# Placing small products behind dense ones, an earlier rotary table, and stores on another queue, in a one-layer hybrid attention and RWKV-7 block

## The chip, the cores and the metric

The kernel runs on one core of a Trainium2 chip. The metric is the device time of one execution in microseconds (us), lower is better. In the text and the rows PE is TensorE, the matrix engine; DVE is VectorE, ACT is ScalarE, POOL is GpSimd and SP is SyncE, which in this kernel only issues transfers. SPq and POOLq are the queues of transfers that SP and POOL issue.

## The reference, cut to what matters

One decoder layer over 1024 tokens of width 1024, in float32. One wide projection of the normed input feeds two token mixers that stand side by side: multi-head latent attention (8 heads, with low-rank queries and keys and a rotary part) and an RWKV-7 recurrence (8 heads of 64). Sixteen blocks of gate columns of the same projection merge them.

```
z = rmsnorm(x, g_mix) @ w_in              # MLA columns | r k v, low-rank w a g | gates
c_q, c_kv, k_pe = split(z_mla)            # 384 | 256 | 32 columns
q  = rmsnorm(c_q) @ w_uq;  kv = rmsnorm(c_kv) @ w_ukv
cos, sin = rope_tables(positions)         # rotary tables, applied to 32 columns of q and k
o_mla = causal_attention(q, k, v) @ w_o_mla

w = decay(w0 + tanh(w_lo) @ w2);  a = sigmoid(a0 + a_lo @ a2);  g = sigmoid(g_lo) @ g2
kk = k * k_k / norm(k * k_k)              # per head
S_t = S_{t-1} diag(decay_t) + (S_{t-1} a_t) b_t^T + v_t k_t^T ;  y_t = S_t r_t
o_rwkv = (groupnorm(y) + bonus) * g @ w_o_rwkv

x = x + sigmoid(gate_1) * o_mla + sigmoid(gate_2) * o_rwkv
x = x + relu(rmsnorm(x) @ w_up)**2 @ w_down
x = x + sigmoid(rmsnorm(x) @ w_gate) * (p @ w_proj);  out = rmsnorm(x) * g_final
```

## The kernel before, in words

Float32 matrices are split into a rounded high part and a low remainder, and each product is taken as three: high by high, low by high, high by low. One block of 128 columns of the wide projection is then 48 products of 128x512, three for each of 8 slices of the inner dimension and two halves of the tokens. These are the **dense** products (tiles `psd`, and `pg` for gate blocks of the recurrence). Around each block the raw weights arrive (`wr`), ACT rounds them (`wh`, line 215), DVE takes the remainder (`wl`, line 216), and at its end ACT and DVE read the block out of the accumulator.

The stages follow one another on PE:

- **First stage** (0 to 143 us of the profiled execution): the norm and transposes of x, the key columns, the low-rank columns, then the low-rank products (`lora`, line 466: 12 results, each read out by ACT into a tile `sa` and stored), then the norm of the keys: `n2`, its square root `sn`, DVE's reciprocal `rn` and a Newton step (lines 477 to 488), rounded by ACT into `rns`. Four small products `nb` (line 502) spread it over the keys, `kz`, which are stored in `kh_d`. Tiles `kz`, `n2`, `sn`, `rn`, `sa`, `zs` share 13 buffers, tag `ta`.
- **Early stage** (143 to 368 us). The generator `early(g)`, for each of 8 groups of 128 tokens, loads what the first stage stored and makes the small products `L` (line 670). `inverse(b)`, for each half of the sequence, loads them as `U` and inverts 32x32 triangles by forward substitution on DVE, a chain of 62 instructions (`prd`, `X`, lines 689 and 690) in which each waits for the one before it. It stores the result, loads it transposed (`mt`), and DVE transposes it once more (`x`, line 707). Then PE runs 128 small products `y` (lines 714 and 722) in 16 groups of 8, ACT copying between the groups. `norm_latent` needs a small product `st`, some DVE arithmetic, and a transpose `rT` (line 293).
- **Recurrence stage** (368 to 590 us): for each of 16 chunks products `pc` in three steps, each followed by a copy or a sum on DVE and ACT that the next step waits for.
- **Attention stage** (590 to 836 us): `latents` loads five stored tiles (`latf`, 512 KB each) and splits them into `chi` and `clo`; `rope_tables` computes the rotary table in 13 DVE instructions and a sine on ACT; then values (`v`), queries (`qp`) and keys (`kn`), and the heads.
- Then the merge (to 1033 us), the channel mixer (to 1660 us), and the gated embedding with the final norm (`gated`, line 1679).

Chunks of work are Python generators that yield an estimate of their cost. `weave` draws from several in turn so that their costs grow in given proportions, and this sets the order of the instructions on every engine. The dense blocks are the filler: `main` (all columns that are still to be made) is woven with the small work at weights `T_EARLY` 203, `T_LATE` 600, `T_MAIN` 306 and `T_REST` 40. A larger number yielded by a small chunk lets more dense products follow it. Each engine works through its own instructions in order. `together` keeps a few small products next to one another. All stores go through SP's queue, which also carries nearly all loads.

```
first = chainit(*(early(g) for g in range(4)))
second = chainit(weave([(inverse(0), 40), (chainit(*(early(g) for g in range(4, 8))), 22)]), inverse(1))
run(weave([(chainit(first, second), T_EARLY), (main, T_MAIN)], lead=True))
```

## Time and profile before

| | |
|---|---|
| median of 3 runs | 1764.86 us (1764.24 to 1766.14) |
| the profiled execution | 1766.65 us, of which the span 1764.9 us |
| PE busy | 1689.4 us, 96% of the span |
| DVE, ACT, POOL busy | 1190.9, 850.9 and 263.6 us |
| mean granted TensorE clock | 0.987 |

PE is the bound: what counts is the time in which it is idle, and the time at a clock below 1.00. Other engines matter where PE waits for them. The granted clock is given as a share of 2.4 GHz; 0.50 is 1.2 GHz.

### The profile page before, as it was taken

To read this page: it belongs to the slowest core of one execution; us is meant where nothing else is said; L and a number is where in the kernel's file an instruction comes from. 1 tells how busy PE (TensorE), PEld (TensorE's weight loads), DVE (VectorE), ACT (ScalarE), POOL (GpSimd) and SP (SyncE) were. 2 spreads that over 40 slices of the span, in tenths; PEclk is the share of its full clock that TensorE was granted. 3 is DMA by queue.
4 is the path that set the end of the run, shared out by engine and by line. 5 is a ranking of instruction groups with operands and counts; after the bars stand their busy time and mean duration, and the time that the engine had idled before them with its cause. 6 is when DMAs were issued, how large, how long until landed. Compare 5 with 4: busy or idle time off the path is not lost.

```text
span 1764.9 us, 27006 instructions
## 1 busy us (share of the span) xinstructions
PE 1689.4 (96%) x10492; PEld 1374.2 (78%) x10492; DVE 1190.9 (67%) x1923; ACT 850.9 (48%) x1482; POOL 263.6 (15%) x206
## 2 busy tenths in 40 slices
PE   7999999889999999998999999999999999999997
PEld 6877877667777877777888887888888888888876
DVE  6446695858777578887364378555658787786656
ACT  5553333244444366676244156555556444353365
POOL 2000000000000022222000203333332333332000
PEclk9999999979999999999999999999999999999999
DMA  6257774744553510015353324545558755462213
GB/s 198 72 199 216 199 213 109 194 110 127 162 143 102 178 44 25 25 61 191 107 165 99 111 115 144 167 133 164 165 181 258 234 167 155 152 189 66 72 42 126
DMA packets 241839, 246.12 MB, mean 139 GB/s; under 512 B 48977, under 2 KB 186800, under 8 KB 241712
## 3 DMA queue, kind: packets, MB, share of 16 engines
q1 hardware_dynamic: 239792, 239.39, 44.3%
q0 software_dynamic: 1760, 4.76, 0.8%
q8 instruction: 82, 1.34, 0.3%
q14 instruction: 45, 0.37, 0.1%
q10 hardware_dynamic: 160, 0.27, 0.0%
HBM read 162.31 MB, written 81.53 MB: 138 GB/s over the span
## 4 chain that ended last, share of the span: by engine, by line
PE 69%; DVE 14%; issue 6%; DMA 4%; ACT 4%; POOL 1%; SPq 1%; DVEq 0%; ACTq 0%; POOLq 0%
PE psX L1394 18%; PE psd L225 18%; PE psY L1394 9%; PE pg L1660 5%; PE psZ L1394 5%; PE pg L610 2%; DVE prd L689 1%; DMA r<-rkv_d 1%; PE po L1147 1%; PE k L234 1%; DVE wl L216 1%; DMA a<-sa_d 1%; DVE xb L319 1%; DVE X L690 1%; PE pT L1130 1%
## 5 line engine op out<-in xcount | busy, mean ns | idle before, releaser
L1394 PE MATMUL psX<-xb,sw 128*128 128x512 f32 x768 | 177.5, 389 | 2.2 <-ACT hid L1497 1.1
L1394 PE MATMUL psX<-hb,sw 128*128 128x512 f32 x768 | 176.8, 389 | 0.0
L1394 PEld LDWEIGHTS psX<-xb,sw 128*128 128x128 f32 x768 | 144.0, 188 | 32.9 <-ACT hid L1497 1.6
L1394 PEld LDWEIGHTS psX<-hb,sw 128*128 128x128 f32 x768 | 144.1, 188 | 29.9
L319 DVE TENSOR_TENSOR sw<-sw,sw 128x512 fp32r<-128x512 f32 x128 | 94.3, 741 | 55.3 <-ACT sw L318 55.0
L318 ACT CAST sw<-sw 128x512 fp32r<-128x512 f32 x128 | 79.4, 620 | 103.7 <-PE psX L1394 37.4
L215 ACT CAST wh<-wr 128x1024 fp32r<-128x1024 f32 (+2 forms) x67 | 57.0, 855 | 139.0 <-PE psd L225 120.6
L225 PE MATMUL psd<-xh,wh 128*128 128x512 f32 x384 | 122.8, 399 | 0.5 <-ACT yn L888 0.5
L225 PE MATMUL psd<-xl,wh 128*128 128x512 f32 x384 | 122.2, 397 | 0.0
L216 DVE TENSOR_TENSOR wl<-wr,wh 128x1024 fp32r<-128x1024 f32 (+2 forms) x67 | 68.2, 1020 | 47.8 <-PE psd L225 29.2
L318 ACT CAST sw<-wr 128x512 fp32r<-128x512 f32 x96 | 59.3, 622 | 72.9 <-PE psX L1394 38.7
L225 PE MATMUL psd<-xh,wl 128*128 128x512 f32 x384 | 92.0, 390 | 0.0
L1660 PE MATMUL pg<-wg,g 128*128 128x512 f32 x384 | 91.2, 393 | 0.0
L319 DVE TENSOR_TENSOR sw<-wr,sw 128x512 fp32r<-128x512 f32 x96 | 82.3, 857 | 12.1 <-ACT sw L318 12.0
L1394 PE MATMUL psY<-xb,sw 128*128 128x512 f32 x384 | 89.6, 389 | 0.0
L1394 PE MATMUL psY<-hb,sw 128*128 128x512 f32 x384 | 89.6, 389 | 0.0
L225 PEld LDWEIGHTS psd<-xh,wh 128*128 128x128 f32 x384 | 72.7, 191 | 17.0 <-ACT yn L888 1.0
L225 PEld LDWEIGHTS psd<-xl,wh 128*128 128x128 f32 x384 | 73.1, 191 | 15.8
L225 PEld LDWEIGHTS psd<-xh,wl 128*128 128x128 f32 x384 | 72.0, 188 | 15.4
L1394 PEld LDWEIGHTS psY<-hb,sw 128*128 128x128 f32 x384 | 72.1, 188 | 15.0
L1394 PEld LDWEIGHTS psY<-xb,sw 128*128 128x128 f32 x384 | 72.1, 188 | 15.0
L318 ACT CAST hb<-braw 128x1024 fp32r<-128x1024 f32 x56 | 58.7, 1048 | 51.1 <-DMA braw<-hid_d 19.1
(411 smaller groups left out, 3743.0 us busy)
## 6 DMA issues: line engine op xcount, KB each, us to landing
hid_d<-hid SPq DMA_DIRECT2D x112, 256.0 KB, 4.2
braw<-hid_d SPq DMA_DIRECT2D x56, 512.0 KB, 4.4
wr<-in_w_in_dram SPq DMA_DIRECT2D x35, 512.0 KB, 5.2
wr<-in_w_ffn_up_dram SPq DMA_DIRECT2D x32, 512.0 KB, 5.1
wr<-in_w_ffn_down_dram SPq DMA_DIRECT2D x32, 512.0 KB, 4.0
gate_d<-gt SPq DMA_DIRECT2D x16, 512.0 KB, 3.1
gate<-gate_d SPq DMA_DIRECT2D x16, 512.0 KB, 3.7
xt<-in_x_dram SPq DMA_DIRECT2D x8, 512.0 KB, 8.3
```

The source lines that it names most:

```text
L215: A.copy(dst(wh), src)
L216: V.tensor_tensor(dst(wl), src, dst(wh).bitcast(F32), ALU.subtract)
L225: T.matmul(acc[:, h, :], lhsT=wt[:, k, :], rhs=r[k][:, h * 512:h * 512 + 512], start=wt is wh and k == 0 and ri == 0, stop=wt is wl and k ...
L234: T.matmul(acc, lhsT=wt[:, k, :], rhs=r[k][:, sl], start=wt is wh and k == 0 and ri == 0, stop=wt is wl and k == kb - 1)
L318: A.copy(hi, src)
L319: V.tensor_tensor(lo, src, hi.bitcast(F32), ALU.subtract)
L610: T.matmul(acc, lhsT=wt[:, k, :], rhs=r[k][:, hs], start=wt is wh and k == 0 and ri == 0, stop=wt is wl and k == NB - 1)
L689: V.tensor_tensor(pv, X[:, 0:t, 0:t], U[:, 0:t, t].unsqueeze(1).to_broadcast([P, t, t]), ALU.mult)
L690: V.tensor_reduce(X[:, 0:t, t], pv, AX.X, ALU.add)
L1130: T.transpose(out=tp_[:, b * P:(b + 1) * P], in_=prs[i][:, (4 * g + b) * P:(4 * g + b + 1) * P], identity=ident)
L1394: T.matmul(acc, lhsT=w[:, wl_, j, :], rhs=part(b, xl_, j), start=start and s == 0, stop=key == LAST[bank] and s == len(steps) - 1, skip_gr ...
L1660: T.matmul(acc, lhsT=l[k][:, ts], rhs=r, start=first and i == 0, stop=last and i == 2)
```

## The change

- **Behind dense products.** `behind_dense()` makes the first of a few small products follow the dense step that was last written ahead of it. `together` uses it, and now also holds the products of `early`, of `inverse` (`y`) and `sc` of the recurrence; the transpose in `norm_latent` uses it too.
- **More dense work ahead of the inverse's products.** `inverse` yields 12 in place of 3 before its products, and a step of the recurrence yields 2 at one place in place of two yields of 1.
- **First stage.** The low-rank products become a generator that is woven with the dense block that followed them, and with the rotary table, which moves here from the attention stage. The table is stored (`tab_d`) and loaded again in attention.
- **Latents.** The statistics of `norm_latent` become `latent_rstd`, with dense work between it and the transpose.
- **Attention.** 26 slots are touched first in another order, the five loads `latf` have a slot each (two before), and `rope_keys` stands ahead of `latents`.
- **Stores.** 104 stores move from SP's queue to POOL's.
- **Tail.** `gated` runs a square root of one column on ACT after its second sigmoid, so that the table of functions is loaded there.

```diff
+    def behind_dense():
+        return tc.issue_after(dense_last[0])
...
     def together(*mms):
-            first = mms[0]()
+            with behind_dense():
+                first = mms[0]()
             with tc.issue_after(first.ins):
                 for f in mms[1:]:
-                    last = f()
-            return last
+                    f()
...
+        def low_rank():
+            for which in range(3):
+                for j in range(4):
...
                     t = ta("sa")
                     if which < 2:
                         A.activation(t, flat(acc), AF.Sigmoid, bias=pcol(("w0", "a0")[which], j))
-                        nc.sync.dma_start(sa_d[which, cs, :], t)
+                        nc.gpsimd.dma_start(sa_d[which, cs, :], t)
...
+                    yield 1.7
+        def rope_tables():
+            freq_sb = cp.tile([P, 3], F32, name="freq_sb")
+            nc.sync.dma_start(freq_sb, freq)
+            posi, kf, ang = ta("posi"), ta("kf"), ta("ang")
+            nc.sync.dma_start(posi.bitcast(I32), positions.broadcast_to([P, S]))
+            yield 1
+            V.tensor_copy(ang, posi.bitcast(I32))
+            V.tensor_scalar(ang, ang, freq_sb[:, 0:1], None, ALU.mult)
...
+            for c in (c1, c2, 2 * math.pi - c1 - c2):
+                V.scalar_tensor_tensor(ang, kf, -c, ang, ALU.mult, ALU.add)
+                yield 1
...
+            with tc.issue_after(lora_last[0].ins):
+                A.activation(ang, ang, AF.Sin)
+            V.tensor_scalar(ang, ang, freq_sb[:, 1:2], None, ALU.mult)
+            nc.sync.dma_start(tab_d, ang[64:128])
...
-        run(dense(w_in, 0, NB, MLA_COLS, RV0 * P, xh, xl, evac_rv))
+        tables = rope_tables()
+        run(weave([(dense(w_in, 0, NB, MLA_COLS, RV0 * P, xh, xl, evac_rv), 20.6), (low_rank(), 24), (until(tables, 8), 8)]))
...
+        run(tables)
...
         def latent_cols():
             q = dense(w_in, 0, NB, 0, QR, xh, xl, evac_c)
             yield from dense(w_in, 0, NB, QR, KVR, xh, xl, evac_c, m0=3)
-            yield from until(q, 12)
-            yield from norm_latent((3, 4), KVR, "g_kv", 0)
+            yield from until(q, 8)
+            r = latent_rstd((3, 4), KVR)
+            yield from until(q, 8)
+            yield from norm_latent(r, (3, 4), "g_kv", 0)
...
             def inverse(b):
...
-                yield 3
+                yield 12
                 for c in range(8):
                     y2 = psa((P, 4, CH), s="y2")
-                    for j in range(4):
-                        for h in range(2):
...
+                    together(*[lambda j=j, Rt=Rt, Rb=Rb: T.matmul(y2[Rb, j, 0:32], lhsT=lr[Rt, c * 4 + j, :], rhs=x0[Rt, c * 4 + j, :], start=True, stop=True)
+                               for j in range(4) for Rt, Rb in tops])
...
                 if next_mms:
                     put_values(Wn)
-                yield 1
+                yield 2
...
-                nc.sync.dma_start(fm(yb_d[0], g), hi.bitcast(F32))
+                nc.gpsimd.dma_start(fm(yb_d[0], g), hi.bitcast(F32))
...
+        for i in (14, 15, 6, 7, 2, 3, 4, 5, 21, 10, 11, 0, 1, 8, 12, 16, 9, 13, 17, 18, 19, 20, 22, 23, 24, 25):
+            slot(i)
...
-                    t = slot((12, 13)[n % 2], F32, "latf")
+                    t = slot((12, 13, 19, 20, 24)[n], F32, "latf")
                     nc.sync.dma_start(t, lat_d[m])
...
-            prep = chainit(latents(), lazy(rope_tables), value_weights(), values(0, V0, psa_v), queries(0, psv))
+            prep = chainit(lazy(rope_keys), latents(), value_weights(), values(0, V0, psa_v), queries(0, psv))
...
             A.activation(t, acc, AF.Sigmoid, scale=r1[tb])
+            if n:
+                A.activation(warm, warm, AF.Sqrt)
```

Three places show how instructions move. Lines are those of the kernel in question.

**The key's norm and the low-rank products, ACT and DVE.** On ACT before, the read-outs `sa` of all low-rank products stand ahead of the norm (`n` and its root `sn`), and the rounding `rns` comes two dense read-outs later:

```order
L472 COPY sa_1015<-lora_1008 128x1024
L472 COPY sa_1025<-lora_1018 128x1024
L478 COPY n_134_1028<-kst_618 8x512
L478 COPY n_134_1028<-kst_619 8x512
L480 ACT_TABLE_LOAD
L480 ACTIVATE sn_1029<-n_134_1028 8x1024
L215 CAST wh_1227<-wr_1225 128x1024
L386 ACTIVATE zs_1098<-psd_1049,omu 128x1024
L215 CAST wh_1353<-wr_1351 128x1024
L487 CAST rns<-rn_1030 8x1024
```

On ACT now, the root stands ahead of all twelve read-outs, and `rns` between the fifth and the sixth:

```order
L531 ACTIVATE sn_926<-n_110_925 8x1024
L215 CAST wh_1250<-wr_1248 128x1024
L490 ACT_TABLE_LOAD
L490 ACTIVATE sa_956<-lora_951,pc_rest 128x1024
L490 ACTIVATE sa_974<-lora_969,pc_rest 128x1024
L490 ACTIVATE sa_994<-lora_989,pc_rest 128x1024
L490 ACTIVATE sa_1010<-lora_1005,pc_rest 128x1024
L490 ACTIVATE sa_1023<-lora_1018,pc_rest 128x1024
L538 CAST rns<-rn_927 8x1024
L490 ACTIVATE sa_1037<-lora_1032,pc_rest 128x1024
L490 ACTIVATE sa_1054<-lora_1049,pc_rest 128x1024
```

On DVE now, instructions of the rotary table (`ang`, `kf`) alternate with those that lead from the reciprocal to the finished `rn`, which `rns` reads:

```order
L532 RECIPROCAL rn_927<-sn_926 8x1024
L504 CAST ang_963<-posi_961 128x1024
L533 TENSOR_TENSOR sn_926<-rn_927 8x1024
L505 TENSOR_SCALAR ang_963<-ang_963,freq_sb 128x1024
L534 TENSOR_TENSOR sn_926<-sn_926,n_110_925 8x1024
L506 TENSOR_SCALAR kf_962<-ang_963 128x1024
L535 TENSOR_SCALAR sn_926<-sn_926 8x1024
L507 TENSOR_SCALAR kf_962<-kf_962 128x1024
L536 TENSOR_TENSOR rn_927<-rn_927,sn_926 8x1024
L512 SCALAR_TENSOR_TENSOR ang_963<-kf_962,ang_963 128x1024
L537 TENSOR_SCALAR rn_927<-rn_927 8x1024
```

Five table instructions now stand between the reciprocal and the end of the norm.

**The second inverse's products, PE.** Before, the 128 products `y` follow 212 dense ones and stand with no dense product among them:

```order
L225 MATMUL psd_2924<-xh_171,wl_2921 128x512 x2
L225 MATMUL psd_2924<-xh_172,wl_2921 128x512 x2
L714 MATMUL y_351_2803<-x_348_2774,lr_2775 32x32
L714 MATMUL y_353_2833<-x_348_2774,lr_2775 32x32
L714 MATMUL y_351_2803<-x_348_2774,lr_2775 32x32 x7
L714 MATMUL y_353_2833<-x_348_2774,lr_2775 32x32 x7
L722 MATMUL y_351_2803<-mt_1198,y2s_2812 32x32 x8
L722 MATMUL y_353_2833<-mt_1198,y2s_2842 32x32 x8
L714 MATMUL y_355_2859<-x_348_2774,lr_2775 32x32 x8
```

Now they follow 281 dense products, and each group of 8 is followed by one to six more:

```order
L231 MATMUL psd_2917<-xh_172,wl_2914 128x512 x2
L231 MATMUL psd_2917<-xh_173,wl_2914 128x512 x2
L231 MATMUL psd_2975<-xh_166,wh_2971 128x512 x2
L231 MATMUL psd_2975<-xl_174,wh_2971 128x512 x2
L765 MATMUL y_369_2980<-x_356_2867,lr_2868 32x32 x8
L231 MATMUL psd_2975<-xh_167,wh_2971 128x512 x2
L231 MATMUL psd_2975<-xl_175,wh_2971 128x512
L774 MATMUL y_369_2980<-mt_1221,y2s_2989 32x32 x8
L231 MATMUL psd_2975<-xl_175,wh_2971 128x512
L231 MATMUL psd_2975<-xh_168,wh_2971 128x512 x2
L231 MATMUL psd_2975<-xl_176,wh_2971 128x512 x2
L765 MATMUL y_371_3010<-x_356_2867,lr_2868 32x32 x8
```

**The loads at the start of attention, SP.** Before, the first two `latf` loads come right after the stores `yb_d` of the recurrence's last result, and PE has 140 dense products between the transposes of that result and the first `v`:

```order
L895 DMA yb_d<-yh_5723 128x4x128
L896 DMA yb_d<-yl_5724 128x4x128
L989 DMA latf_5755<-lat_d 128x1024
L989 DMA latf_5787<-lat_d 128x1024
L943 DMA posi_5889<-in_positions_dram 128x1024
L115 DMA wr_6397<-in_w_ukv_dram 128x2x256
L1038 DMA uq_6576<-in_w_uq_dram 128x3x192
L989 DMA latf_5809<-lat_d 128x1024
```

Now the five stand together behind the load `uq_6606`, which waits for DVE's second `wl` of the weights `wr_6090`, and that for the last dense product of the stage. PE has 18 dense products between those transposes and the first `v`:

```order
L940 DMA g_5903<-g_d 128x4x128
L1070 DMA uq_6606<-in_w_uq_dram 128x3x192
L991 DMA tab_5955<-tab_d 64x1024
L993 DMA kpr_5967<-kpr_d 64x1024
L1021 DMA latf_5980<-lat_d 128x1024
L1021 DMA latf_5994<-lat_d 128x1024
L1021 DMA latf_5998<-lat_d 128x1024
L1021 DMA latf_6002<-lat_d 128x1024
L1021 DMA latf_6006<-lat_d 128x1024
```

The dense products that stood there are among those that now stand earlier.

## Rows read from the trace of the kernel before

**Rows 1.** Windows of PE: us, busy (instructions), granted clock, DMA share, GB/s.

```profile
98.00:117.00 19.00, 17.30 (x68) 0.91 0.80 310
...
345.00:374.00 29.00, 16.37 (x287) 0.59 0.73 173
...
400.00:540.00 140.00, 126.96 (x1684) 1.00 0.55 149
...
621.00:640.00 19.00, 16.81 (x68) 0.91 0.29 85
```

**Rows 2.** Timeline of PE: first low-rank product, and the dense one after the last.

```profile
98.71 0.40 PE L466 MATMUL lora<-lora,lw_h 128*128 128x512 f32 x1
...
116.27 0.63 PE L225 MATMUL psd<-xh,wh 128*128 128x512 f32 x2
```

**Rows 3.** Timeline of PE: 75 products of 128x512 in a row.

```profile
1737.67 17.16 PE L1660 MATMUL pg<-wg,g 128*128 128x512 f32 x75
```

**Rows 4.** Timeline of ACT: the key's norm.

```profile
117.42 1.05 ACT L478 COPY n<-kst 8x512 f32<-8x512 f32 x2
118.49 1.28 ACT L480 ACT_TABLE_LOAD   x1
119.78 1.06 ACT L480 ACTIVATE sn<-n 8x1024 f32<-8x1024 f32 x1
```

**Rows 5.** Timeline of DVE: three instructions of the key's norm.

```profile
120.87 6.54 DVE L481 RECIPROCAL rn<-sn 8x1024 f32<-8x1024 f32 x1 [1.69 <-ACT sn L480]
...
128.59 1.21 DVE L482 TENSOR_TENSOR sn<-rn 8x1024 f32<-8x1024 f32 x1
...
132.16 0.68 DVE L484 TENSOR_SCALAR sn<-sn 8x1024 f32<-8x1024 f32 x1
```

**Rows 6.** Timeline of PE: the transpose of the second latent norm.

```profile
236.42 0.27 PE L293 MATMUL rT<-ident,rr 128*8 128x128 f32 x1 [2.47 <-DVE rr L207]
```

**Rows 7.** Timeline of PE: two groups of `y` in the first inverse, one dense product between.

```profile
289.76 0.44 PE L714 MATMUL y<-x,lr 32*32 32x32 f32 x16
...
290.56 0.44 PE L714 MATMUL y<-x,lr 32*32 32x32 f32 x16
```

**Rows 8.** Timeline of PE: the second inverse's first products.

```profile
354.50 0.42 PE L714 MATMUL y<-x,lr 32*32 32x32 f32 x4 [8.64 <-DVE x L707]
```

**Rows 9.** Window of DVE: the second inverse's chain; columns as in the first group.

```profile
287.00:345.00 58.00, 47.08 (x72) 1.00 0.54 149
```

**Rows 10.** Timeline of DVE: a wait inside that chain, its end, the transpose after it.

```profile
302.44 1.23 DVE L216 TENSOR_TENSOR wl<-wr,wh 128x1024 fp32r<-128x1024 f32 x1 [9.07 <-PE psd L225]
...
343.56 1.16 DVE L690 TENSOR_REDUCE X<-prd 128x31 f32<-128x961 f32 x1
...
355.19 1.24 DVE L707 STREAM_TRANSPOSE x<-xc 32x1024 f32<-32x1024 f32 x1 [0.74 <-ACT xc L706]
```

**Rows 11.** Timeline of PE: two waits of the recurrence stage.

```profile
488.19 0.69 PE L852 MATMUL pc<-W,bk 128*64 128x64 f32 x16 [1.34 <-ACT W L848]
...
535.85 0.69 PE L833 MATMUL pc<-W,q 128*64 128x64 f32 x16 [1.34 <-DVE W L859]
```

**Rows 12.** Timeline of PE: the wait at the start of attention.

```profile
632.04 0.47 PE L234 MATMUL kn<-chi,wh 128*128 128x512 f32 x1 [2.19 <-ACT wh L215]
```

**Rows 13.** Timeline of ACT: the rounding of one latent tile.

```profile
599.58 1.05 ACT L318 CAST chi<-latf 128x1024 fp32r<-128x1024 f32 x1 [0.82 <-DMA latf<-lat_d]
```

**Rows 14.** DMA issues: queue, number, KB each, median us to landing.

```profile
sa_d<-sa SPq DMA_DIRECT2D x8, 512.0 KB, 3.0
...
latf<-lat_d SPq DMA_DIRECT2D x5, 512.0 KB, 5.0
...
bh<-yb_d POOLq DMA_DIRECT2D x4, 512.0 KB, 9.1
```

**Rows 15.** Timeline of ACT: the root of the last block's norm.

```profile
1757.84 1.28 ACT L202 ACT_TABLE_LOAD   x1
1759.14 0.20 ACT L202 ACTIVATE rs<-rv 128x1 f32<-128x1 f32 x1
```

155 lines of the change are left out of this document (76 added, 79 removed).

## The prediction, made before the changed kernel was run

> **What bounds the kernel now.** I read the windows of PE first, then PE's timeline for each window in which it is idle or its granted clock is below 1.00, then the queues of the engines that it waits for there. PE is busy for 96% of the span, so the change can only gain where PE stands still or runs at half clock, and each dense product that fills one hole is taken from another place. The number of dense products is the same before and after. One of them advances PE by 0.227 us, (17.16 - 0.16) / 75 [rows 3].
>
> The windows to look at are four [rows 1]: the low-rank products (clock 0.91), the second inverse (16.37 busy of 29.00 us at 0.59), the recurrence stage (126.96 of 140 us) and the start of attention (16.81 of 19 us at 0.91). All times below are on the scale of the profiled execution, 1766.65 us, 1.8 above the median.
>
> **The change part by part** (+ is time saved).
>
> *Second inverse, +19.* The last dense product ends at 345.9; the first `y` starts after a wait of 8.64 us for DVE's transposes [rows 8], and the clock stays at half to about 373.9: 28.0 us. The work done in them, at full clock, is 256 records of `y` at 0.44 / 16 less their start-up, about 5.9 us [rows 7], ten dense products, 2.3, and 0.5 of transposes: 8.7. The loss is 19.3. Why so late? DVE's chain starts at 287.3, stands 9.07 us behind a `wl` that waits for PE, ends at 344.7, and the second transpose ends at 356.4 [rows 10], 11.7 later (a store, a load, copies on ACT). Of DVE's 47.1 busy us there [rows 9] some 43 are the chain, counting off the other work.
>
> In the new order the chain starts when the last dense block of the `r` columns ends, t. It needs 2.5 us of that block's read-out (`wl` and `zs`), 43 of chain, about 7 of other work put among it: `x` is whole at t + 52 + 11.7 = t + 64. PE has 292 dense products and 24 records of the first inverse before the second's first `y`: t + 68. No wait, with 4 us to spare. I take +19; were DVE 9 us slower, the gain would be +14.
>
> *Visits, -3.6.* Between two groups of `y`, 0.80 us apart, stand 0.37 of `y` and one dense product: the mixing costs 0.20 [rows 7]. In the new order there are about 16 such visits more in the second inverse and 7 in the first: -3.6 to -4.6, and -2 if longer stretches between groups cost less.
>
> *First inverse, -3.5.* Its chain now starts after a transpose `rT`, 51 us after the products `nb` end, and its 43 us have some 28 us of other instructions among them, of which, as between 198 and 268 us before, about three quarters count: the end is at 115, plus 2 for waits, and the first transpose of `x` 8.5 later, at 126. PE arrives at about 124 (264 dense, 32 products for the rotary key columns, the small ones). I take 2 us of waiting and 1.5 of half clock; 0 and -8 are the ends.
>
> *The second `rT`, +3.7.* PE waits 2.47 us there for DVE's `rr` [rows 6] and then runs four us at a clock near 0.57, 1.7 more. The statistics now stand 38 dense products and 16 `L` ahead, 9.8 us, as long as DVE's part took (227.0 to 236.4). Ends: 0 and +4.2.
>
> *Low-rank products, -7.6.* Before, 60 products take 17.6 us [rows 2] where 13.6 would do: 4.0 lost. In the new order ACT's rounding `rns` stands ahead of the sixth read-out, and PE has three accumulators. `rns` needs the end of the key's norm. Count from the end of the last `kst`: two copies, a table load and the root, 3.5 us [rows 4], the reciprocal, 6.5, and then not five but ten instructions on DVE, five of them of the table; at 1.21 or 0.68 each they take 8.9 [rows 5]. `rns` is done 20 us after `kst`. PE in that time has 31 dense products (7.0) and five groups of low-rank ones (about 5.5, plus 1.2 for their read-outs of 1.0 each): it stands some 7 us. Then about 2 us are lost at half clock, and 2 before it: 11.6 in all, against 4.0. If the table's instructions cost nothing, the loss would be 6; if stores hold the buffers of `sa`, 16. So -2 to -12.
>
> *Recurrence, +6.* PE is idle for 13.0 of 140 us [rows 1], in waits of one to one and a half us for the copies after each step [rows 11]. The waits for ACT's `W` had two to four dense products ahead of them, and now mostly ten, or six and four with `sc` between: these go, about 5 us and what is like them. One comes: the transposes `yT` now stand ahead of a step and need DVE's `yc`, which has two instructions of 1.2 us ahead of it. Half of the 13; ends 0 and +13.
>
> *Start of attention, -9.7.* Before, PE waits 2.19 us [rows 12] and loses 1.7 to the clock. Now the five `latf` stand on SP behind a load that waits until 0.6 us after the last dense product, t. Four loads are issued by t + 2.3, all eight by t + 4.7. A `latf` takes 5.0 us to land [rows 14], and the eight are 3.4 MB: at 310 GB/s 11 us, at 173 20 us [rows 1]. ACT rounds each in 1.05 [rows 13], DVE takes three instructions for the rotary key first and then 1.2 for each `clo`. So the first `v` starts near t + 8.6, and the last `clo` is there at t + 18. PE has 27 products to do in that time, 6.1 us: idle for 11.9, then 1.7 at half clock as before. 13.6 against 3.9. Ends: -3 (all landed by t + 9) and -18 (last at t + 22).
>
> *Tail, +0.9.* The table load of 1.28 us between the last sum and the root [rows 15] moves ahead of ACT's last square, into 1.49 us in which ACT waits for DVE.
>
> *Stores, 0.* POOL is idle for nearly all of 150 to 625 us, so issuing costs nothing. What a store on its queue takes is not in the trace of before; the nearest rows are 3.0 us on SP's and 9.1 on POOL's for eight loads issued together [rows 14]. I take the lower: most stores come singly. The waits that hang on them (buffers of `sa`, the reload of `kh_d`, `l_d`) then stay as they were.
>
> The Trainium skill speaks here against the change: by "SBUF — State Buffer", section "SBUF: two separate sides", GpSimd writes the descriptors of its transfers itself, and cannot while certain DVE instructions hold the port that the two share, so that such a transfer seems blocked. By it a store issued beside the reciprocal could start as much as 6.5 us later, and the sum would be that of the third rival below. The row of `bh` neither shows nor excludes it.
>
> **Sum:** 19 - 3.6 - 3.5 + 3.7 - 7.6 + 6 - 9.7 + 0.9 = +5.2. 1766.65 - 5.2 = 1761.4, and 1.8 lower on the scale of the median: 1759.6 us.
>
> **The rivals.**
>
> *The holes move and nothing is gained.* The idle time of PE stays what it was, because the filler is the same: the recurrence gives nothing (DVE's own queue holds each step), and the rest of the sum is -0.8: 1765.7 us. For it: the two new holes above are read off the order alone. Against: the hole at 346 us is nearly all loss at half clock, and 4 us of slack speak for it.
>
> *Slower, by the latent loads.* Eight transfers at 173 GB/s, the last `clo` at t + 26: PE idle for 20 us, -18 in place of -9.7: 1768. From -15 on (a last `clo` after t + 23) it decides. For it: the rate at 345 us; against: 310 GB/s at 98 us.
>
> *Slower, by late stores on POOL's queue.* At 9.1 us a store, the third buffer of `sa` comes 1.4 us later, and `kh_d` to `k` to the first `L` 5 us; -8 with the clock: 1768. It decides where stores take over 7 us. For it: the row of `bh`; against: those eight share the bandwidth.
>
> *Much faster.* `rns` doesn't hold the read-outs because DVE gets to the norm sooner, and the latents land by t + 9: +5.6 and +6.7: 1747.
>
> **How the numbers follow.** My forecast 0.40, much faster 0.14, nothing gained 0.22, the two slower ones 0.14 and 0.10. A measurement of this kernel tells about 0.2%, 3.5 us, from no change. The forecast lies 5 us below the median, so a part of its spread lies within 3.5: faster 0.51, same 0.24, slower 0.25. The range, 1746 to 1772, takes in all cases; the likeliest one's own is 1752 to 1766.
>
> **What would show it right or wrong.** Around the second `y` PE should be busy at clock 1.00, with dense products between the groups. In the first stage a wait of about 7 us for ACT's `sa` or `rns` should stand among the low-rank products. At the start of attention several waits for `chi` and `clo`, 10 to 13 us in all, with `latf` issued after the last gate block's `wl`. `rT` should wait less than 1 us. The waits of `pc` for ACT's `W` should be gone, and `yT` should wait for `yc`. The prediction is wrong if the second inverse still waits, if PE passes the low-rank products without a long wait, or if the latents are there when PE wants them.

## The result, and the profile after

The changed kernel takes **1773.82 us** (median of 4 runs, 1772.71 to 1776.1) against 1764.55 us beside it: a ratio of 1.0052 with an interval of 1.0037 to 1.0067, some 9 us slower. Forecast were 1759.6 us, in a range of 1746 to 1772. The execution profiled after has a span of 1772.5 us (before 1764.9).

The windows of PE that answer to [rows 1], and two in which a new hole stands (us, busy, granted clock, DMA share, GB/s):

```profile
98.00:117.00 19.00, 18.25 (x77) 1.00 0.39 138
122.00:132.00 10.00, 6.04 (x14) 0.50 0.47 170
...
345.00:374.00 29.00, 29.00 (x184) 1.00 0.57 155
400.00:540.00 140.00, 137.65 (x1810) 1.00 0.56 156
607.00:627.00 20.00, 7.21 (x17) 0.57 0.85 279
836.00:852.00 16.00, 11.35 (x35) 0.79 0.77 281
```

The second inverse is full at clock 1.00 (16.37 of 29 us at 0.59 before), and the recurrence has lost nearly all its idle time (137.65 of 140 us, before 126.96). The low-rank products, the start of attention and, at 836 us, the merge have holes, in each of them with a part at 0.50, 1.2 GHz. PE's timeline shows what PE waits for there, and at the products `L` and the transpose `rT` of the early stage:

```profile
125.96 0.80 PE L487 MATMUL lora<-lora,lw_h 128*128 128x512 f32 x1 [6.48 <-ACT sa L490]
...
178.80 1.24 PE L722 MATMUL L<-ah,a 64*64 64x64 f32 x32 [3.40 <-DVE a L717]
...
246.28 0.27 PE L310 MATMUL rT<-ident,rr 128*8 128x128 f32 x1 [3.56 <-DVE rr L207]
...
617.49 1.22 PE L1046 MATMUL v<-wvh,chi 128*128 128x512 f32 x2 [10.45 <-ACT chi L335]
621.04 0.80 PE L1046 MATMUL v<-wvh,clo 128*128 128x512 f32 x1 [2.34 <-DVE clo L336]
...
838.09 1.19 PE L231 MATMUL psd<-bh,wh 128*128 128x512 f32 x4 [0.22 <-DMA bh<-yb_d]
840.91 1.20 PE L231 MATMUL psd<-bl,wh 128*128 128x512 f32 x4 [1.63 <-DMA bl<-yb_d]
843.47 1.18 PE L231 MATMUL psd<-bh,wh 128*128 128x512 f32 x4 [1.36 <-DMA bh<-yb_d]
846.09 2.07 PE L231 MATMUL psd<-bl,wh 128*128 128x512 f32 x4 [1.44 <-DMA bl<-yb_d]
```

For the balance I cut both spans at the same products: the last `nb`, the first and the last `y`, the first `v`, the first `s` (the heads' first product), the first product with `bh` and the first with `oh`. The dense products that fill the stretches were moved between them, so what a stretch saved is its length before, less its length after, plus 0.227 us [rows 3] for each dense product that it now holds more, and less for each that it holds fewer.

| stretch | before, us | after, us | dense products | saved, us | forecast |
|---|---|---|---|---|---|
| start to the last `nb` | 142.5 | 150.8 | 288, 288 | -8.3 | -7.6 |
| to the first `y` | 137.1 | 132.8 | 465, 436 | -2.3 | 3.7 - 2 = +1.7 |
| to the last `y` | 87.9 | 107.3 | 255, 391 | +11.5 | 19 - 3.6 - 1.5 = +13.9 |
| to the first `v` | 253.6 | 226.6 | 568, 469 | +4.5 | |
| to the first `s` | 23.9 | 26.7 | 8, 0 | -4.6 | the two: 6 - 9.7 = -3.7 |
| to the first `bh` | 191.6 | 191.6 | none | 0 | 0 |
| to the first `oh` | 43.6 | 52.3 | none | **-8.7** | 0 |
| to the end | 884.7 | 884.4 | none | +0.3 | +0.9 |
| sum | 1764.9 | 1772.5 | 1584, 1584 | -7.6 | +5.2 |

Of the forecast -3.5 for the first inverse, 2 us are a wait that ends with the first `y`, so they stand in the row before. Two rows make up the miss of 12.8 us: the merge, which the prediction did not look at, with 8.7, and the stretch up to the first `y` with 4.0. The misses of the other rows cancel, which is luck.

### The profile page after: what moved, and what is told of

The parts are those of the page before. It is cut to its first block, busy times and chain, and to the rows that moved or that the text cites. A ratio compares the mean times of both kernels' runs of the same rounds, so it can differ in the third digit from the quotient of the medians.

```text
span 1772.5 us, 27095 instructions
## 1 busy us (share of the span) xinstructions
PE 1695.8 (96%) x10492; PEld 1371.0 (77%) x10492; DVE 1189.1 (67%) x1923; ACT 853.5 (48%) x1491; POOL 329.0 (19%) x312
## 4 chain that ended last, share of the span: by engine, by line
PE 65%; issue 18%; DVE 9%; DMA 3%; ACT 2%; POOL 2%; SPq 0%; DVEq 0%; POOLq 0%; ACTq 0%
PE psd L231 19%; PE psX L1426 18%; PE psY L1426 9%; PE pg L1692 5%; PE psZ L1426 5%; PE po L1179 2%; PE pT L1162 1%; PE k L241 1%; DVE nmx L1138 1%; DVE xb L336 1%; PE qp L241 1%; DMA bl<-yb_d 1%; PE s L1132 1%; PE s L1133 1%; PE s L1134 1%
## 5 line engine op out<-in xcount | busy, mean ns | idle before, releaser
L231 PE MATMUL psd<-xh,wl 128*128 128x512 f32 x384 | 97.0, 399 | 0.0
L1348 POOL TENSOR_TENSOR sw<-wr,wr 128x512 f32<-128x512 f32 x32 | 49.7, 1554 | 223.8 <-DVE sw L336 87.4
L336 DVE TENSOR_TENSOR sw<-wr,sw 128x512 fp32r<-128x512 f32 x96 | 81.1, 845 | 12.0 <-ACT sw L335 11.8
L231 PEld LDWEIGHTS psd<-xl,wh 128*128 128x128 f32 x384 | 73.3, 191 | 16.2
L336 DVE TENSOR_TENSOR hb<-braw,hb 128x1024 fp32r<-128x1024 f32 x56 | 78.2, 1396 | 8.3 <-ACT hb L335 8.2
```

The source lines that it names most:

```text
L231: mm = T.matmul(acc[:, h, :], lhsT=wt[:, k, :], rhs=r[k][:, h * 512:h * 512 + 512], start=wt is wh and k == 0 and ri == 0, stop=wt is wl a ...
L336: V.tensor_tensor(lo, src, hi.bitcast(F32), ALU.subtract)
L1348: G.tensor_tensor(s1, a21, a22, ALU.add)
```

## The experiments

The runs were made in five groups (e, f, g, h and i), each beside runs of the kernel before, whose medians lie between 1762.9 and 1765.4 us. So runs of different groups compare best by their ratios. All times and ratios to the kernel before:

| run | median, us | ratio | interval |
|---|---|---|---|
| the changed kernel | 1773.82 | 1.0052 | 1.0037 to 1.0067 |
| e1, merge's tiles off prob | 1765.66 | 1.0000 | 0.9990 to 1.0011 |
| e2, kernel before with the new slots | 1769.84 | 1.0022 | 1.0009 to 1.0036 |
| e3, all stores on SP | 1777.79 | 1.0068 | 1.0043 to 1.0093 |
| e4, rns behind the read-outs | 1770.27 | 1.0034 | 1.0021 to 1.0047 |
| f1, five kinds of stores on SP | 1771.57 | 1.0044 | 1.0028 to 1.0059 |
| f3, inverse undone | 1773.40 | 1.0063 | 1.0042 to 1.0085 |
| f4, latents first | 1773.13 | 1.0057 | 1.0039 to 1.0074 |
| f5, latents first, new slots, merge | 1758.50 | 0.9970 | 0.9956 to 0.9984 |
| g1, low-rank products undone | 1774.59 | 1.0066 | 1.0048 to 1.0084 |
| g2, f5 with g1 and the tail | 1758.72 | 0.9974 | 0.9964 to 0.9985 |
| g3, f5 with e4 and the tail | 1757.70 | 0.9963 | 0.9949 to 0.9977 |
| g4, g2 with f1 | 1760.71 | 0.9993 | 0.9977 to 1.0008 |
| h1, f5 with stores by stage | 1750.63 | 0.9936 | 0.9913 to 0.9959 |
| h2, f5 without the table's arithmetic | 1749.28 | 0.9921 | 0.9904 to 0.9939 |
| h3, h1 with e4 | 1750.13 | 0.9929 | 0.9911 to 0.9946 |
| i1, h1 with the table later | 1744.58 | 0.9893 | 0.9876 to 0.9911 |

And what each stretch saved against before, in us, worked out as in the table above:

| stretch to | after | e1 | e3 | e4 | f1 | f3 | f4 | f5 | g1 | h1 | h2 | i1 |
|---|---|---|---|---|---|---|---|---|---|---|---|---|
| last `nb` | -8.3 | -6.6 | -6.9 | -2.9 | -7.2 | -6.7 | -6.7 | -6.6 | -1.6 | -7.2 | +1.3 | +1.2 |
| first `y` | -2.3 | -6.3 | +5.6 | -3.8 | -2.2 | -4.7 | -6.4 | -4.8 | -10.0 | +5.0 | -5.1 | +4.4 |
| last `y` | +11.5 | +11.6 | +6.7 | +11.6 | +12.4 | +0.4 | +11.6 | +11.6 | +11.7 | +10.9 | +11.5 | +9.8 |
| first `v` | +4.5 | +3.6 | -7.6 | +3.6 | +4.8 | +13.5 | +6.4 | +12.0 | +4.7 | +12.2 | +12.5 | +12.1 |
| first `s` | -4.6 | -3.0 | -2.8 | -4.2 | -5.4 | +2.6 | -3.7 | -4.0 | -3.9 | -3.2 | -3.2 | -3.1 |
| first `oh` | -8.7 | 0.0 | -7.5 | -6.8 | -8.6 | -9.9 | -7.3 | -0.1 | -8.0 | 0.0 | +0.1 | 0.0 |

After, e1, f4 and f5 have the same code up to the first `y` and differ in that row by up to 4 us between executions, so a difference of that size or less in one execution settles nothing there.

**The merge (e1, e2).** POOL's timeline shows when the eight loads are issued that the first merge products need, after:

```profile
830.80 0.59 POOL L1238 DMA_DIRECT2D bh<-yb_d  x1 [25.74 <-DVE probT L1167]
...
834.53 0.59 POOL L1239 DMA_DIRECT2D bl<-yb_d  x1
```

Before, they were issued from 805.75 to 810.1 us. They wait for the last head because `bh` is claimed first in its pool, and the new order of the slots puts slots 14 and 15, which hold `prob`, on that memory. e1 claims the merge's tiles in another order:

```diff
+        for n in ("r0", "r1", "a8", "a9", "a10", "a11", "a12", "a13", "a14", "r2", "r3", "a15"):
+            rslot(int(n[1:]), "res") if n[0] == "r" else aslot(int(n[1:]))
         bh, bl = [aslot(8 + i, F32R, "bh") for i in range(4)], [aslot(12 + i, F32R, "bl") for i in range(4)]
```

> The changed kernel, with the merge stage's tiles claimed in an order that puts its first two residual tiles, and not the first two tiles of bh, on the memory of attention slots 14 and 15 (prob). Theory A (placement): the bh and bl loads wait for the last head's prob tiles only because the new slot order puts them on that memory. Then GpSimd issues them near 805 us instead of 830.8, the first bh product waits no more than before, the stretch from the first bh to the first oh product falls from 52.3 to about 44 us, and the time from 1773.8 to about 1765.5 us. Theory B (queue): they are late because of the stores that now go through GpSimd's queue; then they stay near 831 us and the time stays at 1773.8.

POOL's timeline in e1:

```profile
806.48 0.59 POOL L1240 DMA_DIRECT2D bh<-yb_d  x1
...
810.83 0.54 POOL L1241 DMA_DIRECT2D bl<-yb_d  x1
```

The loads go out at 806.48 us, the stretch takes 43.6 us as before, and the time is that of the kernel before. Theory A holds with its number. e2 turns it round, in the kernel before:

```diff
+        for i in (14, 15, 6, 7, 2, 3, 4, 5, 21, 10, 11, 0, 1, 8, 12, 16, 9, 13, 17, 18, 19, 20, 22, 23, 24, 25):
+            slot(i)
         lat = [(slot(2 * m, F32R, "chi"), slot(2 * m + 1, F32R, "clo")) for m in range(5)]
```

> The kernel before, with nothing but the new order in which attention's slots are claimed (its stores all stay on SP's queue). Theory A: bh and bl are issued near 830 us in place of 806, the merge stage takes 8 us longer, and the time goes from 1764.6 to about 1772 us, give or take 2 us for what the placement does at the start of attention. Theory B: bh stays near 806 us and the time at 1764.6.

In its profile the loads go out at 821.78 us and the stretch takes 50.1 us, 6.5 more: the placement alone does it. The whole time rose by 4.4 us, less than the 8 expected. The profiled execution (1763.97 us) was the fastest of ten, so its other stretches, left out of the table, say little.

**The stores (e3, f1).** e3 puts every moved store back (`nc.gpsimd.dma_start` to `nc.sync.dma_start`, 15 places).

> The changed kernel with all its fifteen kinds of moved stores back on SP's queue. Theory A: bh stays near 831 us, the merge stage at 52 us. The waits of L for DVE's a (3.4 us) and of rT (3.56 us) may change by a few us either way, as SP's queue holds loads behind stores; 1770 to 1780 us. Theory B: bh goes back to 806 us and the time falls by 8 us to about 1766. Should the stores on GpSimd's queue be what makes kh_d, and with it the first L, late, the two L waits of 4.0 us in all fall to 1 and the time by 3 us.

The merge stays late (theory B falls), and the stores prove to be no zero but two large terms of opposite sign. Up to the first `y` the kernel with all stores on SP saves 5.6 us where the changed kernel loses 2.3: the wait of `rT` is gone and `L` waits 1.4 us. Waits of SP's queue in the changed kernel, 150 to 300 us (us in total, times, longest), and landing times of its stores:

```profile
SPq L708 <- DMA cum_d<-sw: 10.8, 3, 5.3
SPq L708 <- DMA kh_d<-kz: 10.3, 1, 10.3
SPq L708 <- DMA ah_d<-ah: 8.7, 4, 5.8
```

```profile
cum_d<-sw POOLq DMA_DIRECT2D x8, 256.0 KB, 5.3
...
l_d<-lt POOLq DMA_DIRECT2D x16, 128.0 KB, 4.1
```

On SP's queue the two landed in 3.2 and 3.0 us before. In the changed kernel the next group's loads wait on SP for the landing of `cum_d` and `ah_d`, whose buffers they fill.

The queue of a store also changes something that the edit does not name: the order in which the same instructions stand on PE. Counted from the last `nb`:

| | before | after | f5 | e3 | h1 |
|---|---|---|---|---|---|
| dense products ahead of the second, third, fourth `L` | 27, 18, 29 | 15, 14, 13 | 15, 14, 13 | 27, 18, 29 | 27, 18, 29 |
| DVE has the third `a`, us | 29.2 | 27.9 | 29.6 | 27.0 | 27.3 |
| DVE has the first `x`, us | 133.8 | 132.0 | 134.2 | 131.0 | 132.1 |
| first `y` starts, us | 137.1 | 132.8 | 135.2 | 131.5 | 132.1 |
| dense products up to it | 465 | 436 | 436 | 465 | 465 |

The third `L` waits 3.40 us in the changed kernel (the row at 178.80 us above) and not at all in h1 (described below):

```profile
177.09 1.15 PE L722 MATMUL L<-ah,a 64*64 64x64 f32 x32
```

DVE has its `a` within 0.6 us of the same time in both, counted from the last `nb`; PE comes to it some 3 us earlier in the changed kernel, with 29 dense products in place of 45 since the first `L`. And the first `y` starts within 1.3 us of the same time in the changed kernel, e3 and h1, but in e3 and h1 PE has done 29 dense products more by then, 6.6 us. So a large part of what the stores cost here lies in the order. No run changes the queue and keeps the order, so the part of the later landing is not known.

In the recurrence it is the other way: with the stores on SP the stretch to the first `v` loses 7.6 us, on POOL it saves 4.5. In h1, where of the stores of those stages only `gate_d` and `yb_d` are on POOL, it saves 12.2, as in f5. In e3, from 400 to 600 us, SP waits with stores in hand for their data, and DVE for loads; of the waits there, DVE's row first and then two of SP's:

```profile
DVE a L810 <- DMA a<-sa_d: 13.4, 5, 4.0
```

```profile
SPq L668 <- ACT gt L667: 37.4, 6, 11.8
SPq L944 <- ACT yh L335: 36.3, 5, 9.1
```

The loads of `a` stand behind them, and DVE waits 13.4 us for these (11.8 in the kernel before); in the changed kernel it does not wait for them there at all. The Trainium skill, "DMA: Bandwidth & Descriptors", section "Issuing engines are not separate DMA queues", says that issuing transfers from several engines saves only the sequencer's time to issue, usually little. These runs differ: what was saved is the time in which a store that waits for its data holds up the loads behind it, and PE's idle time from 400 to 600 us is 10.7 us in e3 and 2.45 in the changed kernel.

f1 puts only `kh_d`, `cum_d`, `ah_d`, `bh_d` and `l_d` back on SP.

> The changed kernel with five kinds of stores back on SP's queue: kh_d and the four of the second stage (cum_d, ah_d, bh_d, l_d). The others, those of the recurrence among them, stay on GpSimd's. Theory: with all stores on SP the second stage was 8 us shorter and the recurrence 12 us longer, because in the second stage loads into the same buffers wait for stores that land later from GpSimd's queue, and in the recurrence loads stood on SP behind stores that waited for their data. Then here the stretch from the last nb product to the first y gains about 8 us (with 0.227 us for each dense product more or less in it), L waits about 1.4 us and rT nothing, while the recurrence keeps its gain: 1765 to 1768 us. Rival: the gain of the recurrence needs the second stage's stores off SP too, or the second stage's loss comes from the other stores (rkv_d, sa_d, lat_d); then the time stays within 3 us of 1773.8.

`L` and `rT` wait 2.3 and 0.6 us as expected, and the order of `L` is that of before. But a read-out `zs` on DVE now holds PE for 4.2 us, so that the stretch saves no more than in the changed kernel, and the time is the rival's. That read-out, at 277.76 us, stands right behind the end of the inverse's chain, which comes 128.1 us after the last `nb`, in h1 122.6. Two instructions of the recurrence (`a`, at 264.17 and 266.31 us) stand among the chain here, the first after a wait of 1.54 us for a load, and in h1 they stand behind it. So `cum_d`, `ah_d`, `bh_d`, `l_d` and `kh_d` on SP do not give the stretch back; h1 below moves the other stores of the two stages as well. The recurrence kept its gain.

**The first stage (e4, g1).** ACT's and DVE's timelines there, after:

```profile
116.12 2.12 ACT L490 ACTIVATE sa<-lora,pc_rest 128x1024 f32<-128x1024 f32 x2 [0.90 <-DMA sa_d<-sa]
123.85 1.04 ACT L538 CAST rns<-rn 8x1024 fp32r<-8x1024 f32 x1 [5.61 <-DVE rn L537]
124.80 2.10 ACT L490 ACTIVATE sa<-lora,pc_rest 128x1024 f32<-128x1024 f32 x2
```

```profile
109.13 6.54 DVE L532 RECIPROCAL rn<-sn 8x1024 f32<-8x1024 f32 x1 [1.69 <-ACT sn L531]
115.60 0.62 DVE L504 CAST ang<-posi 128x1024 f32<-128x1024 int32 x1
116.14 1.20 DVE L533 TENSOR_TENSOR sn<-rn 8x1024 f32<-8x1024 f32 x1
117.27 0.73 DVE L505 TENSOR_SCALAR ang<-ang,freq_sb 128x1024 f32<-128x1024 f32 x1
```

This is the picture that the prediction drew: `rns` ahead of the sixth read-out, and instructions of the table (`ang`) among those of the norm. e4 takes `rns` away from there:

```diff
-        A.copy(rns[0:H], rn)
-        V.tensor_tensor(rns[32:32 + H], rn, rns[0:H].bitcast(F32), ALU.subtract)
...
         run(weave([(dense(...), 20.6), (low_rank(), 24), (until(tables, 8), 8)]))
+        with tc.issue_after(lora_last[0].ins):
+            A.copy(rns[0:H], rn)
+        V.tensor_tensor(rns[32:32 + H], rn, rns[0:H].bitcast(F32), ALU.subtract)
```

> The changed kernel with the rounding of the key's norm (rns, on ACT) queued behind the last read-out of the low-rank products; the table's instructions stay where they are. Theory: PE's wait of 6.48 us at the low-rank products is there only because rns stands ahead of the sixth read-out on ACT. Then that wait goes, with it the stretch at half clock behind it, the first nb product starts 7 to 9 us earlier (near 138 us instead of 146.4), and the time is about 1766 us. Rival: the first stage is late because the low-rank products now share PE and read-outs with dense ones; then the wait only moves to another read-out, and the gain is under 3 us. Should the second stage be bound by DVE's chain towards the first inverse (tables and norm included), part of the gain comes back as waits of L or y: 1768 to 1771.

The wait of 6.48 us becomes one of 3.1 for `zs` on DVE and several for `sa`, 1.8 in all. The first stage gets back 5.4 us of its 8.3, of which `L` and `rT` take some (3.7 and 4.5 us of waits). g1 puts the low-rank products back in one block (`run(low_rank())` ahead of the norm, and without them in the `weave`).

> The changed kernel with the low-rank products back in one block ahead of the dense block, as before; the table's instructions stay in the first stage. Theory: the mixing is what costs the first stage its 8.3 us (rns and the read-outs behind it on ACT, zs on DVE, the clock after that); without it the last nb product starts 5 to 8 us earlier than in the changed kernel (143 to 146 us in place of 150.8), and the time is 1766 to 1769 us. Rival: the table's fourteen instructions on DVE, put among the norm's, are what costs it; then nb gains under 3 us and the time stays at 1771 or more.

The last `nb` comes at 144.1 us, as the theory says, but all of it is given back before the first `y` (-10.0 us). The time doesn't fall, which was to speak for the rival, the table on DVE; but by the rival `nb` was to gain under 3 us, and it gained 6.7. So this run decides for neither. From PE's waits between 90 and 400 us:

```profile
PE L L723 <- DVE a L718: 5.8, 2, 3.8
PE rT L310 <- DVE rr L207: 3.3, 1, 3.3
```

**The second inverse (f3).**

```diff
-                yield 12
+                yield 3
                 for c in range(8):
...
-                    together(*[... T.matmul(y2[Rb, j, 0:32], ...) ...])
+                    for j in range(4):
+                        for h in range(2):
...
+                            T.matmul(y2[Rb, j, 0:32], lhsT=lr[Rt, c * 4 + j, :], rhs=x0[Rt, c * 4 + j, :], start=True, stop=True)
```

> The changed kernel with the inverse's part undone: the pause after its table is 3 again and its first products stand in plain order, not behind a dense one. Theory: the part as a whole (no wait, no half clock at the second inverse, more visits) is worth 11.5 us between the first and the last y, as predicted; PE again waits 7 to 10 us for DVE's x there and runs at half clock for 20 us, and the dense products that it no longer takes go to the recurrence and to the start of attention, where they fill 4 to 8 us of the hole: 1777 to 1781 us. Rival: the hole only moves, and what is lost at the inverse comes back at the start of attention: 1773.8 within 3.

The hole at the inverse comes back (a wait of 6.6 us for `x`, 11.1 us of the saving gone), and the hole at the start of attention is filled: PE is busy in 48.05 of the 50 us from 600 to 650, against 34.99. The stretches from the last `y` to the first `s` save 16.2 us more. The rival holds: in the changed kernel the inverse's gain was paid for with the dense products that attention lacked.

**The start of attention (f4, f5).** SP's and ACT's timelines, after:

```profile
607.71 0.37 SPq L1070 DMA_DIRECT2D uq<-in_w_uq_dram  x1
...
609.55 4.18 SPq L1021 DMA_DIRECT2D latf<-lat_d  x5
```

```profile
614.06 1.14 ACT L335 CAST wvh<-wr 128x512 fp32r<-128x512 f32 x2 [6.39 <-DMA gate_d<-gt]
616.39 1.04 ACT L335 CAST chi<-latf 128x1024 fp32r<-128x1024 f32 x1 [1.20 <-DMA latf<-lat_d]
```

f4 puts the five loads first:

```diff
-                    nc.sync.dma_start(t, lat_d[m])
+                    latf_last[0] = nc.sync.dma_start(t, lat_d[m])
...
+                    with tc.issue_after(latf_last[0].ins) if h == 2 else ExitStack():
                         nc.sync.dma_start(raw, w_uq[...])
...
-            prep = chainit(lazy(rope_keys), latents(), value_weights(), ...)
+            prep = chainit(latents(), lazy(rope_keys), value_weights(), ...)
```

> The changed kernel with the five latf loads ahead of the weight load (uq) that waits for the last gate block's rounding, and of the rotary key's loads. Theory A, the loads are what is late: latf land near 609 us in place of 616, the first v starts 5 to 6 us earlier, 1768. Theory B, two things end within 2 us of each other: ACT's wvh ahead of chi waits for the store of the last gate tile (614.06 us, it stands on that tile's memory), so the first v starts only 1.2 us earlier (about 616.3), though the later clo no longer wait: 1770 to 1772.5.

```profile
615.85 1.14 ACT L335 CAST wvh<-wr 128x512 fp32r<-128x512 f32 x2 [5.91 <-DMA gate_d<-gt]
616.89 3.88 ACT L335 CAST chi<-latf 128x1024 fp32r<-128x1024 f32 x4
```

Theory B: four `chi` now run without a wait, but behind `wvh`, and PE's wait falls only from 10.45 to 8.67 us. `wvh` stands on slot 14, on the memory of the last gate tile, whose store on POOL's queue must land first. f5 moves that too, and takes e1 in:

```diff
-        for i in (14, 15, 6, 7, ..., 20, 22, 23, 24, 25):
+        for i in (25, 22, 6, 7, ..., 20, 14, 23, 24, 15):
```

> As the run before, and attention's slots 25 and 22 (late value tiles) instead of 14 and 15 (wvh, wvl and later prob) on the first two places, with the merge stage's tiles claimed so that bh and bl stand on no prob tile. Theory: wvh no longer waits for the gate tile's store, the first v starts near 611 us (6 us earlier than in the changed kernel), and the merge stage takes 43.6 us: 1773.8 - 8.2 - 6, about 1759 to 1761 us. Rival: the hole at the start of attention is set by something else behind it (clo on DVE, the read-outs vt, the rotary key); then the gain there stays under 2 us and the time is about 1764.

```profile
610.70 1.22 PE L1048 MATMUL v<-wvh,chi 128*128 128x512 f32 x2 [2.66 <-ACT chi L335]
```

That is PE's timeline in f5. The wait is 2.66 us, and the time 1758.5 us, half a microsecond under what was expected and faster than the kernel before.

**Combinations (g2, g3, g4).** g2 adds g1's edit and, like the other two, the tail as it was meant; g3 adds e4's and puts the table's store on POOL's queue; g4 is g2 with f1's stores.

```diff
-            A.activation(t, acc, AF.Sigmoid, scale=r1[tb])
+            sg = A.activation(t, acc, AF.Sigmoid, scale=r1[tb])
             if n:
-                A.activation(warm, warm, AF.Sqrt)
+                with tc.issue_after(sg.ins):
+                    A.activation(warm, warm, AF.Sqrt)
```

> The run with the latents first and the new slots (1758.5 us), with the low-rank products back in one block, and the root's table load at the end queued behind the sigmoid that it follows in the program. From it the low-rank part 5 to 7 us and the end 0.9 us: 1751 to 1753 us, some 12 us faster than the kernel before. Rival: the gain of the first stage is taken back by later waits of L and rT for DVE (the chain towards the first inverse is bound by DVE): 1756 to 1758.

> The run with the latents first and the new slots (1758.5 us), with the low-rank products still mixed but rns behind their last read-out, the table's store on GpSimd's queue, and the root's table load at the end behind its sigmoid. From it 3.5 us for rns and 0.9 us at the end: 1753 to 1755 us. The store of the table no longer holds SP's queue for 19.7 us; if the loads of the second stage (sw, k, a) waited for that, L's waits fall by 1 to 3 us more.

> The combined kernel with the low-rank products undone, and the stores of kh_d and of the second stage back on SP's queue. Theory: L and rT wait less (2.3 and 0.6 us in place of 4 to 6 and 3.5), 2 to 4 us faster than the combined kernel: 1748 to 1751. Rival: as in the run with these stores alone on SP, a read-out that then waits (4.2 us for zs) takes it back: 1752.

None is measurably faster than f5. g2 comes near its rival; g3 and g4 are slower than any of their forecasts. In g2 `L` and `rT` wait 6.9 and 4.2 us, but that is not all: in the profiled executions the first two stretches together are 1.3 us better than in f5 in g2 and 2.1 in g3. The tail takes this back, for it costs instead of saving: the stretch from the first `oh` to the end loses 3.0 and 2.0 us in g2 and g3, where f5 gained 0.4. In g2 the last root needs no table load, but from the last gate product to the end are 11.4 us in place of 10.5; ACT has 24 table loads after 1650 us in place of 14. g4 waits 8.1 us at `L` and 5.0 at the inverse besides; its profiled execution, 1768.76 us, is the slowest of twelve.

**The two causes apart (h1, h2, h3, i1).** h1 is f5 with every store of the first two stages (the early stores) on SP and those of `gate_d` and `yb_d` alone on POOL.

> The run with the latents first and the new slots (1758.5 us), with all stores of the first and second stage (rkv_d, sa_d, g_d, kh_d, lat_d, kpr_d, cum_d, ah_d, bh_d, l_d) back on SP's queue; only the gates' and the recurrence's (gate_d, yb_d) stay on GpSimd's. Theory A, the stores: the stretch up to the first y, which lost 11.4 us against before, loses 1 to 3, L and rT wait 1.4 and 0 us, the recurrence keeps its gain, and the time is 1749 to 1752 us. Theory B, the table on DVE: the stretch keeps most of its loss, as with only five kinds of stores on SP, and the time stays within 3 us of 1758.5.

h2 is f5 with the table's arithmetic left out:

```diff
-            V.tensor_scalar(ang, ang, freq_sb[:, 0:1], None, ALU.mult)
...
-                V.tensor_tensor(ang, ang, kf, ALU.add)
-                yield 1
             V.tensor_scalar(ang, ang, 3.1415925, -3.1415925, ALU.min, ALU.max)
```

> The run with the latents first and the new slots (1758.5 us), with eleven of the rotary table's fourteen instructions on DVE left out (the cast and the clamp ahead of the sine stay, so the table holds wrong values and the attention is not the reference's). Theory A, the stores: the wait at the low-rank products falls from 6.48 to about 3, by what the table's instructions hold up rns, and L and rT keep their waits (4 to 6 and 3.5 us): 1755 to 1757. Theory B, the table: DVE gets to everything after it about 10 us earlier, the stretch up to the first y loses 3 us in place of 11.4, and the time is about 1750.

Both gained, 7.9 and 9.2 us by the medians and 6 and 9 by the ratios, and in different stretches. h1 saves 5.0 us up to the first `y` where f5 lost 4.8, with the first stage as before it (-7.2). h2 saves 1.3 us up to the last `nb` where f5 lost 6.6, and the second stretch stays (-5.1). In h2 PE's wait at the low-rank products is all but gone. But its order differs too: on ACT `rns` stands behind the eighth read-out `sa`, in the changed kernel and h1 behind the fifth. ACT's timeline in h2:

```profile
118.77 2.12 ACT L490 ACTIVATE sa<-lora,pc_rest 128x1024 f32<-128x1024 f32 x2 [0.33 <-ACT sa L490]
...
122.58 1.05 ACT L523 CAST rns<-rn 8x1024 fp32r<-8x1024 f32 x1 [0.68 <-DVE rn L522]
```

DVE has finished `rn` at 122.54 us there, only 1.3 us earlier than in the changed kernel (123.81). PE's waits in h2, then in h1, from 90 to 400 us:

```profile
PE L L707 <- DVE a L702: 3.7, 2, 3.6
PE rT L310 <- DVE rr L207: 3.7, 1, 3.7
...
PE lora L487 <- ACT sa L490: 0.5, 2, 0.2
```

```profile
PE lora L487 <- ACT sa L490: 7.5, 3, 7.0
...
PE L L722 <- DVE a L717: 1.6, 3, 1.0
```

So neither theory excludes the other: the loss of the first stage comes with the table, that of the second with the stores, and each brings another order with it.

> The run with the stores by stage, with rns behind the last read-out of the low-rank products and the table's store on GpSimd's queue. Theory A: from 1749 to 1752 us of the run before it another 3.5 us as that mend gave alone (1773.8 to 1770.3): 1746 to 1749, 16 to 18 us faster than the kernel before. Theory B: the gain of the first stage is lost again at L and rT, and the time is that of the run with the stores by stage within 1.5 us.

h3 is h1 within 1.5 us: theory B's number, though not at its place. `L` waits 2.8 us and `rT` not at all; the profiled execution, the slowest of six, saves 6.6 us in the stretch to the last `y` where h1 saves 10.9. i1 has h1's stores, computes the whole table behind the last transpose of the second inverse, and stores it on POOL's queue:

```diff
-        run(weave([(dense(...), 20.6), (low_rank(), 24), (until(tables, 8), 8)]))
+        run(weave([(dense(...), 20.6), (low_rank(), 24)]))
...
-            V.tensor_copy(ang, posi.bitcast(I32))
+            with tc.issue_after(x0_last[0].ins):
+                V.tensor_copy(ang, posi.bitcast(I32))
...
+                    if b == 1:
+                        next(tables, None)
                     yield 1
```

> The run with the stores by stage (1750.6 us), with the rotary table computed on DVE behind the last transpose of the second inverse, where DVE is busy for 3.7 of 20 us, instead of in the first stage. If the two causes add up, the first stage loses nothing against before (it lost 7.2 us), the second keeps its gain, and the time is 1742 to 1745 us, 19 us faster than the kernel before. If the first stage's gain is given back at L or at the first inverse, because DVE's chain sets them, it is 1748 to 1751. If the table is late for the first steps of the recurrence, waits of PE for DVE's q or W of 2 to 4 us stand near 390 us: 1746.

The two add up: +1.2 and +4.4 us in the two stretches, 1744.58 us, 1.07% faster than the kernel before (interval 0.89 to 1.24%). Here `rn` is finished at 123.91 us, no earlier than in the changed kernel, and `rns` stands behind the ninth read-out. What costs PE its 6.48 us is thus the place of `rns` among the read-outs, and hardly the time that the table's instructions take from the norm.

## Why the prediction was wrong, step by step

- **Left out: the merge.** The prediction followed the new order of the slots to the five `latf` and no further. It put the merge at nothing; the merge costs 8.7 us after, since the loads of `bh` and `bl` wait for the last head's `prob`, and e1 gives this back whole. This is the largest error, and by itself turns a forecast of 5 us faster into slower.
- **"Stores, 0", and with it "The second `rT`, +3.7".** These failed together, and they are the second largest error. The waits that hang on the stores did not "stay as they were". The stretch up to the first `y` lost 2.3 us (up to 6.4 in other executions of the same code) where +1.7 was forecast, and `rT` waits 3.56 us in place of 2.47 [rows 6], not less than 1. h1, which has the early stores on SP, saves 9.8 us there against f5. What is shown is that the queue of the early stores makes this loss. How is open between two things that go together: stores that land up to 2 us later on POOL's queue, with loads that wait for them, and the order of PE, which has 29 dense products fewer ahead of the first `y`. The third rival named the later landing, with -8 us and a chance of 0.10; but it put the loss at the first `L`, which doesn't wait in the changed kernel, and "where stores take over 7 us", and the medians are 3.3 to 5.3.
- **"Recurrence, +6".** Right in sign, too small: idle time from 400 to 540 us fell from 13.0 to 2.35 us. The waits for ACT's `W` are gone, and `yT` waits for `yc`, as forecast, but for 0.9 us in all. Most of the reason was not in the prediction: the stores that left SP's queue. With them still on SP (e3), 10.7 of the 200 us from 400 to 600 are idle, with them on POOL 2.45, before 13.75.
- **"Start of attention, -9.7".** Too small: from the last dense product to the first `v` PE stands 10.45 us, where 8.6 were forecast, and 2.34 more for `clo`, and the clock stays at 0.50 to 626 us. The loads came some 2 us later than the estimate said, with the last `clo` at 20.7 us in place of 18, although they moved at 332 to 418 GB/s and not at 173. That `wvh` waits for the last gate's store was missed: in the changed kernel `wvh` could start at 614.06 us and the first `latf` landed at 616.31, so both ended within some 2 us, and f4 and f5 had to mend both.
- **"Second inverse, +19", "Visits, -3.6", "First inverse, -3.5".** Together +11.9 forecast, and +11.5 measured up to the last `y`. The sum is right, its parts are not. PE waits nowhere between 280 and 392 us, and the clock is 1.00. So the first inverse costs nothing there: `x` was whole 132.0 us after the last `nb`, not 126, but PE came at 132.8, not 124, after its waits at `L` and `rT`. If the hole was worth its 19 us, the visits cost 7.5; no run measures the two apart. But the rival "the holes move and nothing is gained" was right of this part: f3 shows that without it the same dense products fill attention's hole.
- **"Low-rank products, -7.6".** Measured -8.3, and the wait of 6.48 us is the forecast "some 7 us", at the forecast place. Its parts add up to 11 us and not to 11.6, which changes little. But the cause was shared out wrongly. Without the table's instructions the term was to be -2, because `rn` would come some 4.5 us earlier. h2 and i1 measure +1.3 and +1.2, and there `rn` comes 1.3 us earlier or not at all; `rns` then stands behind more of the read-outs.
- **"Tail, +0.9".** It didn't happen: nothing holds the eight roots where the program writes them, and they run at the start of the kernel, so that the last block loads its table as in [rows 15]:

```profile
L1718 ACT ACTIVATE warm<-warm x8: 186/203/203, 3.0 to 5.6; 128x1 f32<-128x1 f32 x8
```

```profile
1765.41 1.28 ACT L202 ACT_TABLE_LOAD   x1
1766.71 0.20 ACT L202 ACTIVATE rs<-rv 128x1 f32<-128x1 f32 x1
```

What stays open: whether the inverse's part still pays in i1, where attention's hole is mended otherwise; and what the early stores on POOL's queue would cost with the order of PE kept.

## What to carry to other kernels

When a pool's tiles are claimed in a new order, follow each moved tile to the next pool that takes its memory, and read there which loads go out first and who held those bytes last. A queue is moved stage by stage: a store that waits for its data belongs off the queue of the loads, but where loads reuse the buffer that a store empties, a later landing can be paid on the path. After such a move compare the order of the instructions as well: here the same program with other queues had other numbers of dense products between its small ones. Filler that closes one hole is taken from another; so add up the filler, and give the stretch that loses it its own cover before counting the gain.
